# Two-layer hybrid attention trunk on one core: last feed-forward weights kept for the second token group, conditions loaded at their first use, the output projection's second half reversed, GpSimd taken out of the layer change

## The chip, the core and the metric

The kernel runs on one core of a Trainium2 chip. The metric is the device time of one execution in microseconds (us). Before the change the median of three runs is 1992.61 us (1989.99 to 1995.05). One more execution was recorded by the hardware profiler; all rows quoted in this document as "before" come from it.

The engines are named as in the profile: PE is TensorE (PEld is its loading of weights, PEq its sequencer), DVE is VectorE, ACT is ScalarE, POOL is GpSimd, and SP is SyncE, whose queue issues nearly all of this kernel's DMAs, one after another.

## The reference

A trunk of two layers works on 512 latent tokens (a grid 64 wide) and 256 context tokens, of width 1024, in float32. One layer computes:

```
mod            = silu(c) @ w_mod + b_mod          # six vectors: shift, scale, gate, twice; the same from c_ctx for context
h              = rms_norm(x, norm1) * (1 + sc1) + sh1
qa,ka,va, gq,gk,gv, ga,gb = split(h @ w_in)       # 8 windowed heads; 8 query, 2 key/value heads; two gates
ya             = windowed attention(qa, ka, va; + context keys, + position bias)
yb             = attention(rope(norm(gq)), rope(norm(gk)), gv; + context keys)
x              = x + g1 * ((sigmoid(ga) * (ya @ w_pa) + sigmoid(gb) * (yb @ w_pb)) @ w_o)
a, u           = split((rms_norm(x, norm2) * (1 + sc2) + sh2) @ w_ffn_in)      # 2816 columns each
x              = x + g2 * ((silu(a) * u) @ w_ffn_out)
```

Latent queries read their own keys and all context keys in one softmax; context tokens go through the same weights, and their result is needed up to the keys and values of the second layer. A last RMS norm follows.

## The kernel before, in words

**Products.** PE's fast float32 form keeps fewer bits than float32, so each operand is split into a high and a low part, and each product is made of three (high by high, high by low, low by high; `steps`, L369 to L381, the matmuls at L377). A weight comes through `weight` (L356): `raw` loads it in one DMA on the SP queue into one of four buffers `wr`, ACT copies the high part `wh` (L362), and DVE or POOL subtracts it to leave the low part `wl` (L364). There are three buffers each for `wh` and `wl`. A weight block of 1024 columns is 512 KB; eight blocks of 128 rows make one output block (24 matmuls for 512 tokens). Larger tiles live in a pool of 45 equal slots of 128 by 768 (`slot`, `spool`).

**Stages of a layer.** `mixing` makes the projections and attention; `merge` makes the gates (a projection each with weights from `win`) and the two branch projections (`pp`); `out_proj` multiplies by w_o (`po`, L1582 on) and adds to `x`; then the norm before the feed-forward; `ffn`; and `following`, the norm of the next layer. In layer 0 the spans hold latent and context tokens, in layer 1 latent ones alone.

**Order of the work.** In `mixing` PE's order is written out by a planner. It keeps a clock in us, knows what the other engines owe (`go` charges an operation to an engine; `plan["load"]` is the lead given to a weight), and picks between attention's own steps and projections that fill the gaps (`fill` in the two dictionaries, one for each layer). A step can state the time from which it may run (`Until`), and `ready["h"]` is that time for the context half of `h`. The other engines' instructions, and the whole order outside `mixing`, come from a scheduler which lays the instructions out by a simulation of its own, in the order in which the code issues them unless an operand is late.

**The layer change.** Layer 1 has the context's norm still to do when its latent tokens are ready. The leading projections (`prologue`) are the grouped keys (`late_k`), the first two query heads (`gqa_q` 0) and the grouped values (`late_v`), for latent tokens first. The weights of keys and values come through `kept` (L1253), which splits them in two pieces on ACT and DVE each into four of the eight `pt` tiles that attention uses later for the transposed probabilities; there they stay until context's turn. `late_norm` then makes the context half of `h` (L1284 sets its time), after which keys and values of the context follow. Other weights come through `load` (L759): in layer 1 it takes DVE for the subtraction as long as the planner's clock is below 8, and POOL afterwards. The rotary step (L770 to L776) multiplies by the cosine and adds on DVE, and multiplies by the sine on POOL (L774). The normalised keys are split on DVE (L1335); L799 is an ACT pass that empties a PSUM bank.

**The border to `merge`.** `run` calls `conditions` (L424 to L431) ahead of `merge`: it loads the condition vector, spread over 128 partitions (`crow`, 512 KB; two of them in layer 0), and applies silu with one ACT pass and two DVE passes (L435 to L437). The first gate weight and the `yb` tiles, which attention wrote to memory, are loaded after it. The users of `crow` are `mod_one` (L442): one block of `w_mod` each, loaded into a `wr` buffer, multiplied and summed on DVE (L446). In layer 0 blocks 16 and up are made beside `merge`, `out_proj` and `ffn`, those of layer 1 (0 to 39) beside layer 0's `ffn`; in layer 1 only blocks 40 to 47 are left, beside its own `ffn`.

**The output projection** (L1577) takes the tokens in two halves. Each half goes over the eight output blocks j = 0 to 7, and both load and split all eight weights. After the first half its norm and its cuts for the feed-forward (`modulate_half`, `cut`) run on DVE and ACT beside the second half; `late` does the second half's norm, and the feed-forward's first products run beside that.

**The feed-forward** makes its first product with fewer multiplications by sums of quarters (`quad`, matmuls at L1682, weights split at L1573 and L1574, and the first blocks plain, `pf`). The second product goes by chunks of hidden blocks; the last chunk, of six, is done for one group of tokens after another (L1814 to L1829), so that the norm of the first group can begin while the second runs: tokens 0 to 512 and 512 to 768 (context) in layer 0, 0 to 256 and 256 to 512 in layer 1. Each group goes over the eight output blocks and loads and splits all eight weights of 384 KB.

Of the kernel before, what the change touches and what calls it, by code (L numbers as in the profile page):

```python
# [42 lines left out]
for _n in ORDER:  # L43
    for _j in range(COLS[_n][1]):
# [27 lines left out]
         busy=12, ctx=0.0, vat=(1, 1), load=2, qt=2, rx=2, slow=(1.1, 1.2, 1), banks="gst", lead=(2, 1, 2)),  # L72
# [3 lines left out]
         busy=2, ctx=1, vat=(1, 1), load=2.5, qt=2, rx=1, slow=(1, 1, 1), banks="tsg", lead=(2, 2, 1)),  # L76
# [251 lines left out]
class Trunk:  # L328
# [430 lines left out]
    def load(self, l, what, j):  # L759
        if l == 0 and (what, j) in (("gk", 0), ("gv", 0), ("gq", 0)):  # L760
            return None
        first = l == 1 and (not self.flow or self.flow.clock < 8.0)
        return self.weight(self.d["win"][l, BLOCK[what, j]], D, self.nc.vector if first else None)
# [6 lines left out]
    def rope(self, t, pool):  # L770
# [3 lines left out]
        nc.gpsimd.tensor_tensor(sh, sh, self.sin, op=ALU.mult)  # L774
# [478 lines left out]
    def kept(self, l, what):  # L1253

        nc = self.nc
        raw = self.raw(self.d["win"][l, BLOCK[what, 0]], D)
        hi, lo = [[self.att.tile([P, S], F32R, tag="pt", name=self.name(n)) for _ in range(2)] for n in ("kh", "kl")]
        for i in range(2):
            part = raw[:, i * S : i * S + S]
            nc.scalar.activation(hi[i], part, AF.Copy)  # L1260
            nc.vector.tensor_tensor(lo[i], part, hi[i][:].bitcast(F32), op=ALU.subtract)
        return Pieces(hi), Pieces(lo)

    def late_norm(self, l, h, at):
# [19 lines left out]
        self.ready["h"] = end  # L1284
# [7 lines left out]
    def late_k(self, l, h, pool, out):  # L1292

        nc = self.nc
        w = self.kept(l, "gk")
# [45 lines left out]
    def late_v(self, l, h, pool, out):  # L1341

        nc = self.nc
        w = self.kept(l, "gv")
# [22 lines left out]
    def mixing(self, l, h, last, at, todo, spare):  # L1367
# [12 lines left out]
        with ExitStack() as stack:  # L1380
# [5 lines left out]
            pool = self.att = _Bufs(pool_, dict(rx=plan["rx"], qt=plan["qt"], p=ATT_P, pt=ATT_PT))  # L1386
            if at.rest:
# [189 lines left out]
    def out_proj(self, l, merged, x, nh, pool, beside):  # L1577

        hf = [self.slot("hf") for _ in range(KB)]
        right = {}  # L1580
        for half in range(2):
            a, b = half * nh, half * nh + nh  # L1582
            acc = None
            for j in range(KB):
                w = self.weight(self.d["wo"][l, j], D, self.nc.vector)
# [144 lines left out]
    def ffn(self, l, right, late, x, spans, groups, nh, done, pool, beside):  # L1730
# [83 lines left out]
        chunk = (FB - LAST) // CHUNK  # L1814
        for a, b in groups:
            acc = None
            for j in range(KB):
                w = self.weight(d["wfo"][l, j, :, chunk * CHUNK * P :], LAST * P, nc.vector)
# [12 lines left out]
    def run(self):  # L1831
# [3 lines left out]
        with (  # L1835
# [23 lines left out]
            for l in range(DEPTH):  # L1859
# [7 lines left out]
                with (  # L1867
# [6 lines left out]
                    crow, junk = self.conditions(stack.enter_context(  # L1874
                        tc.tile_pool(name=f"c{l}", bufs=1, reuse_waits="tile")), 1 if last else 2)
                    one = lambda l, n: lambda: self.mod_one(l, n, crow, junk)
# [265 lines left out]
```

## Time and profile before

| what | value |
|---|---|
| median of three runs | 1992.61 us |
| profiled execution | 1994.68 us |
| its span, first to last instruction | 1992.9 us |
| mean granted PE clock | 0.990 |
| busy: PE, DVE, ACT, POOL | 97%, 75%, 48%, 12% of the span |
| moved by DMA | 220.31 MB, 111 GB/s |
| loads of w_o, of 512 KB | 32 |
| loads of the feed-forward's last weights, of 384 KB | 32 |
| loads of `crow`, of 512 KB | 3 |

A group's row names line, engine and operation, the output and the inputs by the program's names, the tile's shape and the count; then, after the bar, its busy time, the mean time of one in ns, and the idle time of the engine just before, with the instruction that ended it. A row in order of time starts with the start in us and the busy time. A row of the table by stretch starts with the two ends and the length; busy us and counts of the engines follow, then the granted clock (1.00 is full speed) and the DMA engines' share. A row of the waits names who waits for whom, then total us, the number of waits and the longest. The mean clock of 0.990 and PE's 97% are averages over stages; the holes are short and lie at the borders of stages.

### The profile page before, as it was taken

How to read it: one execution, taken by the hardware profiler on the slowest of the kernel's cores; microseconds unless marked ns; L12 is line 12 of the kernel's file. 1: busy time of each engine (PE TensorE's matmuls, PEld its weight loads, DVE VectorE, ACT ScalarE, POOL GpSimd, SP SyncE). 2: the span in 40 equal slices, each digit the busy share in tenths (PEclk: the TensorE clock that was granted, in tenths of full speed). 3: DMA queues.
4: the chain of work that ended last, by engine and by line, in shares of the span. 5: the costliest groups of instructions: out<-in, count | busy, mean ns of one | idle time of the engine just before them, and what ended most of it. 6: DMA issues, size and time to landing. Idle time of an engine off the chain costs nothing.

```text
span 1992.9 us, 31834 instructions
## 1 busy us (share of the span) xinstructions
PE 1932.7 (97%) x12330; PEld 1785.3 (90%) x12330; DVE 1499.2 (75%) x2827; ACT 963.6 (48%) x1860; POOL 232.2 (12%) x135
## 2 busy tenths in 40 slices
PE   8999999999999999999999998999989999999998
PEld 8989999888899999998999877889978989999997
DVE  7477887789679989787756676889455579867786
ACT  4466666642236524242424354666443455444554
POOL 0332222223200000000000031322300000000000
PEclk9999999999999999999999999999989989999999
DMA  8121112244462343546222521112123543333334
GB/s 320 43 59 51 49 59 62 75 148 164 150 236 85 107 146 104 162 150 199 64 85 70 158 91 43 46 48 80 59 88 111 186 148 117 115 97 107 96 114 130
DMA packets 74839, 220.31 MB, mean 111 GB/s; under 512 B 8896, under 2 KB 11072, under 8 KB 74688
## 3 DMA queue, kind: packets, MB, share of 16 engines
q1 hardware_dynamic: 74688, 218.28, 33.6%
q8 instruction: 97, 1.59, 0.3%
q14 instruction: 54, 0.44, 0.1%
HBM read 206.19 MB, written 6.82 MB: 107 GB/s over the span
## 4 chain that ended last, share of the span: by engine, by line
PE 58%; DVE 10%; DMA 5%; issue 3%; ACT 2%; POOL 0%; SPq 0%; DVEq 0%; POOLq 0%; ACTq 0%
PE po L377 18%; PE qu L1682 10%; PE pj L377 10%; PE qv L1682 5%; PE pp L377 4%; DMA wr<-wmodT 3%; PE pf L377 3%; PE qc L1682 2%; PE pv L940 1%; DVE w L1574 1%; DMA wr<-wfi 1%; DVE wr L446 1%; PE sc L1023 1%; PE y L1059 1%; PE tp L1049 1%
## 5 line engine op out<-in xcount | busy, mean ns | idle before, releaser
L362 ACT ACTIVATE wh<-wr 128x512 fp32r<-128x512 f32 (+2 forms) x233 | 197.7, 852 | 368.8 <-PE po L377 126.7
L1682 PE MATMUL qu<-r,w 128*128 128x384 f32 (+1 forms) x1872 | 293.2, 310 | 1.4 <-ACT tt L1689 1.2
L1682 PEld LDWEIGHTS qu<-r,w 128*128 128x128 f32 x1872 | 279.6, 189 | 5.7 <-ACT tt L1689 5.3
L377 PE MATMUL pj<-h,wh 128*128 128x512 f32 (+1 forms) x688 | 254.1, 369 | 12.3 <-ACT wh L362 8.3
L377 PE MATMUL pj<-h,wl 128*128 128x512 f32 (+1 forms) x688 | 243.9, 355 | 0.0
L377 PE MATMUL pj<-hl,wh 128*128 128x512 f32 (+1 forms) x688 | 243.8, 354 | 0.0
L1573 ACT ACTIVATE w<-wr 128x512 fp32r<-128x512 f32 x234 | 144.1, 626 | 119.9 <-PE po L377 26.2
L377 PE MATMUL po<-ph,wh 128*128 128x512 f32 (+1 forms) x576 | 197.7, 344 | 1.1 <-ACT wh L362 1.1
L377 PE MATMUL po<-ph,wl 128*128 128x512 f32 (+1 forms) x576 | 196.5, 342 | 0.3 <-DVE wl L364 0.2
L364 POOL TENSOR_TENSOR wl<-wr,wh 128x1024 fp32r<-128x1024 f32 (+1 forms) x68 | 151.0, 2223 | 392.9 <-ACT wh L362 392.8
L377 PE MATMUL po<-pl,wh 128*128 128x512 f32 (+1 forms) x576 | 196.2, 341 | 0.0
L364 DVE TENSOR_TENSOR wl<-wr,wh 128x512 fp32r<-128x512 f32 (+2 forms) x165 | 149.4, 910 | 43.2 <-ACT wh L362 37.7
L1574 DVE TENSOR_TENSOR w<-wr,w 128x512 fp32r<-128x512 f32 x234 | 158.4, 686 | 24.0 <-ACT w L1573 22.6
L377 PEld LDWEIGHTS pj<-h,wh 128*128 128x128 f32 x688 | 131.3, 191 | 27.5 <-ACT wh L362 8.7
L1682 PE MATMUL qv<-r,w 128*128 128x384 f32 (+1 forms) x936 | 151.2, 310 | 3.9 <-DVE tt L1996 3.9
L1564 DVE SCALAR_TENSOR_TENSOR x<-po,G,x 128x256 f32<-128x256 f32 (+3 forms) x168 | 98.1, 595 | 67.9 <-PE po L377 67.5
L377 PEld LDWEIGHTS pj<-h,wl 128*128 128x128 f32 x688 | 130.8, 190 | 18.4
L1682 PEld LDWEIGHTS qv<-r,w 128*128 128x128 f32 x936 | 140.9, 189 | 5.6 <-DVE tt L1996 5.5
L377 PEld LDWEIGHTS pj<-hl,wh 128*128 128x128 f32 x688 | 131.4, 191 | 13.6
L499 POOL TENSOR_TENSOR rs<-rs,expo 128x2 f32<-128x2 f32 (+2 forms) x8 | 6.8, 855 | 1133.0 <-DVE rs L498 1133.0
L999 ACT ACTIVATE pth<-tp 128x512 fp32r<-128x512 f32 x176 | 103.6, 595 | 66.3 <-PE tp L1049 37.6
L1000 DVE TENSOR_TENSOR ptl<-tp,pth 128x512 fp32r<-128x512 f32 x176 | 119.8, 685 | 15.1 <-ACT pth L999 13.4
(241 smaller groups left out, 4323.4 us busy)
## 6 DMA issues: line engine op xcount, KB each, us to landing
wr<-wfi SPq DMA_DIRECT2D x88, 512.0 KB, 3.3
wr<-wmodT SPq DMA_DIRECT2D x86, 512.0 KB, 3.4
wr<-win SPq DMA_DIRECT2D x68, 512.0 KB, 3.3
wr<-wo SPq DMA_DIRECT2D x32, 512.0 KB, 4.0
wr<-wfo SPq DMA_DIRECT2D x64, 256.0 KB, 2.7
wr<-wfo SPq DMA_DIRECT2D x32, 384.0 KB, 3.3
wr<-wp SPq DMA_DIRECT2D x32, 256.0 KB, 3.3
x<-x SPq DMA_DIRECT2D x16, 384.0 KB, 7.6
```

The costliest lines, as they stand in the source:

```text
L362: nc.scalar.activation(hi, raw, AF.Copy)
L364: (eng or nc.gpsimd).tensor_tensor(lo, raw, hi[:].bitcast(F32), op=ALU.subtract)
L377: nc.tensor.matmul(ps[:, : b - a], u[:, c], v[k][:, a:b], start=(k == 0 and i == 0), stop=(k == nk - 1 and i == 2),)
L446: nc.vector.tensor_tensor_reduce(w, w, crow[:, 0], 1.0, 0.0, ALU.mult, ALU.add, self.mod[l][:, 0, n : n + 1])
L940: nc.tensor.matmul(ps[:, t * 256 : t * 256 + 256], a[k][:, tok], b[:, c], start=(k == 0 and i == 0), stop=(k == KB - 1 and i == 2))
L999: nc.scalar.activation(hi, tp, AF.Copy)
L1000: nc.vector.tensor_tensor(lo, tp, hi[:].bitcast(F32), op=ALU.subtract)
L1023: nc.tensor.matmul(s[:, lo:up], qt[:, b * P : (b + 1) * P], kk[k][:, lo:up], start=(k == 0 and (b % 2 == 0 or lo > 0)), stop=(k == 1), ski ...
L1564: self.nc.vector.scalar_tensor_tensor(x[j][:, f:u], ps[:, f - a : u - a], self.G[l][i][:, s, j : j + 1], x[j][:, f:u], op0=ALU.mult, op1=A ...
L1573: nc.scalar.activation(t[:, :n], src, AF.Copy)
L1574: nc.vector.tensor_tensor(t[:, n : 2 * n], src, t[:, :n].bitcast(F32), op=ALU.subtract)
L1682: nc.tensor.matmul(banks[bank], u[:, c], v, start=(first and k == 0 and i == 0), stop=(k == kn - 1 and i == 2), skip_group_check=True)
```

## The change

Five edits:

- **Last feed-forward weights.** The eight weights of the last chunk are loaded and split for the first group only, into 16 of the 45 slots, and the second group uses them again.
- **Conditions.** `conditions` is no longer called ahead of `merge` but by the first `mod_one` after it: in layer 0 that is still in `merge`, in layer 1 it is in the feed-forward.
- **Output projection.** The second half goes from j = 7 down to 0. The weights 7, 6 and 5 of the first half are still in their buffers and are used again; 4 to 0 are loaded and split a second time.
- **GpSimd.** Each plan gets `quiet`: as long as the planner's clock is below it, the weights loaded through `load` and the sine product of the rotary step take DVE in place of POOL. In layer 1 it is 18, in layer 0 it is 0.
- **Kept tiles.** In layer 1 `spared=2` sends the first two weights that are loaded with a planner (gq1 and gb0) through `kept` into `pt` tiles, and `kept` now charges its passes to the planner. The grouped keys and values take the ordinary buffers `wh` and `wl` instead. The time from which the context half of `h` may be read is put 2.0 us later.

```diff
--- before.py
+++ after.py
@@ -69,11 +69,11 @@
     dict(fill=("nk0 nv0 nq0 gq1 gb0 gq2 gb1 gq3 gb2 gb3 nq1",
                "gb4 nk1 gb5 nq2 nk2 nv1 nq3 nk3 gb6 gb7"),
          early=0.9, reserve=8, hop=0.14, move=3.5, soon=0.5, keep=2,
-         busy=12, ctx=0.0, vat=(1, 1), load=2, qt=2, rx=2, slow=(1.1, 1.2, 1), banks="gst", lead=(2, 1, 2)),
+         busy=12, ctx=0.0, vat=(1, 1), load=2, qt=2, rx=2, slow=(1.1, 1.2, 1), banks="gst", lead=(2, 1, 2), quiet=0.0, spared=0),
     dict(fill=("gq1 gb0 nq0 nv0 gq2 gb1 gq3 gb2 nq1 nk0 gb3",
                "nk1 nk2 nq2 nv1 nk3 gb4 nq3 gb5 gb6 gb7"),
          early=0.8, reserve=2, hop=0.2, move=3, soon=0, keep=2,
-         busy=2, ctx=1, vat=(1, 1), load=2.5, qt=2, rx=1, slow=(1, 1, 1), banks="tsg", lead=(2, 2, 1)),
+         busy=2, ctx=1, vat=(1, 1), load=2.5, qt=2, rx=1, slow=(1, 1, 1), banks="tsg", lead=(2, 2, 1), quiet=18.0, spared=2),
 ]
 
 
@@ -759,7 +759,10 @@
     def load(self, l, what, j):
         if l == 0 and (what, j) in (("gk", 0), ("gv", 0), ("gq", 0)):
             return None
-        first = l == 1 and (not self.flow or self.flow.clock < 8.0)
+        if self.flow and self.spared:
+            self.spared -= 1
+            return self.kept(l, what, j)
+        first = l == 1 and (not self.flow or self.flow.clock < self.quiet)
         return self.weight(self.d["win"][l, BLOCK[what, j]], D, self.nc.vector if first else None)
 
     def go(self, *ops, at=None):
@@ -771,7 +774,7 @@
         nc = self.nc
         sh = self.att.tile([P, T], F32, tag="rx", name=self.name("sh"))[:, :S]
         nc.vector.stream_shuffle(sh, t[:, :S], [i ^ 1 for i in range(32)])
-        nc.gpsimd.tensor_tensor(sh, sh, self.sin, op=ALU.mult)
+        (nc.vector if self.flow.clock < self.quiet else nc.gpsimd).tensor_tensor(sh, sh, self.sin, op=ALU.mult)
         nc.vector.tensor_tensor(t[:, :S], t[:, :S], self.cos, op=ALU.mult)
         nc.vector.tensor_tensor(t[:, :S], t[:, :S], sh, op=ALU.add)
 
@@ -1250,15 +1253,16 @@
         return [self.gqa_k(l, h, joint, pool, at.kk), self.gqa_v(l, h, joint, pool, at.vv),
                 self.gqa_q(l, 0, h, spans, pool, at.gqs)]
 
-    def kept(self, l, what):
-
-        nc = self.nc
-        raw = self.raw(self.d["win"][l, BLOCK[what, 0]], D)
+    def kept(self, l, what, j):
+
+        nc = self.nc
+        raw = self.raw(self.d["win"][l, BLOCK[what, j]], D)
         hi, lo = [[self.att.tile([P, S], F32R, tag="pt", name=self.name(n)) for _ in range(2)] for n in ("kh", "kl")]
         for i in range(2):
             part = raw[:, i * S : i * S + S]
             nc.scalar.activation(hi[i], part, AF.Copy)
             nc.vector.tensor_tensor(lo[i], part, hi[i][:].bitcast(F32), op=ALU.subtract)
+        self.go(("a", D), ("v", D), at=self.flow.clock + self.plan["load"])
         return Pieces(hi), Pieces(lo)
 
     def late_norm(self, l, h, at):
@@ -1281,7 +1285,7 @@
             first = self.go(("v", CTX), at=end if k == 0 else None)
             end = self.go(("a", CTX), ("v", CTX), at=first)
         flow.took("t", first)
-        self.ready["h"] = end
+        self.ready["h"] = end + 2.0
 
     def rest_ready(self):
 
@@ -1292,7 +1296,7 @@
     def late_k(self, l, h, pool, out):
 
         nc = self.nc
-        w = self.kept(l, "gk")
+        w = self.load(l, "gk", 0)
         yield Until(0.0)
         kg = pool.tile([P, T], F32, tag="qt", name=self.name("kg"))
         sq = pool.tile([P, T], F32, tag="qt", name=self.name("sq"))
@@ -1341,7 +1345,7 @@
     def late_v(self, l, h, pool, out):
 
         nc = self.nc
-        w = self.kept(l, "gv")
+        w = self.load(l, "gv", 0)
         yield Until(0.0)
         vt = pool.tile([P, T], F32, tag="qt", name=self.name("vt"))
 
@@ -1384,6 +1388,8 @@
                     tc.tile_pool(name=f"ps{w}{l}", bufs=1, space=PSUM, reuse_waits="tile")) for w in plan["banks"]}
             pool_ = stack.enter_context(tc.tile_pool(name=f"att{l}", bufs=1, reuse_waits="tile"))
             pool = self.att = _Bufs(pool_, dict(rx=plan["rx"], qt=plan["qt"], p=ATT_P, pt=ATT_PT))
+
+            self.quiet, self.spared = plan["quiet"], plan["spared"]
             if at.rest:
                 todo = self.prologue(l, h, spans, spare, at)
                 for g in todo:
@@ -1577,12 +1583,15 @@
     def out_proj(self, l, merged, x, nh, pool, beside):
 
         hf = [self.slot("hf") for _ in range(KB)]
-        right = {}
+        right, ws = {}, {}
         for half in range(2):
             a, b = half * nh, half * nh + nh
             acc = None
-            for j in range(KB):
-                w = self.weight(self.d["wo"][l, j], D, self.nc.vector)
+            for j in range(KB)[:: 1 - 2 * half]:
+
+                if half == 0 or j < KB - 3:
+                    ws[j] = self.weight(self.d["wo"][l, j], D, self.nc.vector)
+                w = ws[j]
                 if half == 0 and beside and MODS[2][j]:
                     beside.pop(0)()
                 ps = self.ps("a", "po")[:, :nh]
@@ -1812,10 +1821,13 @@
             beside.pop(0)[1]()
 
         chunk = (FB - LAST) // CHUNK
+        kept, slots = [], _Bufs(None, {}, dict(we=self.spool))
         for a, b in groups:
             acc = None
             for j in range(KB):
-                w = self.weight(d["wfo"][l, j, :, chunk * CHUNK * P :], LAST * P, nc.vector)
+                if a == 0:
+                    kept.append(self.weight(d["wfo"][l, j, :, chunk * CHUNK * P :], LAST * P, nc.vector, slots))
+                w = kept[j]
                 ps = self.ps("a", "po")[:, : b - a]
                 drain(self.steps(ps, w, second[chunk], a, b, LAST))
                 self.residual(l, 1, ps, x, j, a, b)
@@ -1871,9 +1883,15 @@
                 ):
                     self.psum = dict(n=psn, a=psa)
                     slots = dict(acc=self.spool, sq=self.spool, u=self.spool)
-                    crow, junk = self.conditions(stack.enter_context(
-                        tc.tile_pool(name=f"c{l}", bufs=1, reuse_waits="tile")), 1 if last else 2)
-                    one = lambda l, n: lambda: self.mod_one(l, n, crow, junk)
+                    rows, conds = [], stack.enter_context(tc.tile_pool(name=f"c{l}", bufs=1, reuse_waits="tile"))
+
+                    def one(of, n):
+                        def run():
+                            if not rows:
+                                rows.extend(self.conditions(conds, 1 if last else 2))
+                            self.mod_one(of, n, *rows)
+                        return run
+
                     ahead = 40 if last else 16 + sum(sum(m) for m in MODS)
                     beside = [] if last else [one(0, n) for n in range(16, ahead)]
                     with tc.tile_pool(name=f"m{l}", bufs=1, reuse_waits="tile") as pool_:
```

## The prediction

> **What bounds the kernel.** I read the engines' busy time, then the table by stretch, then the waits, then the order of time where the table shows a hole. TensorE (PE) carries the kernel:
>
> ```profile
> span 1992.9 us, 31834 instructions
> PE 1932.7 (97%) x12330; PEld 1785.3 (90%) x12330; DVE 1499.2 (75%) x2827; ACT 963.6 (48%) x1860; POOL 232.2 (12%) x135
> ...
> 560.00:580.00 20.00, 20.00 (x118) 20.00 (x117) 16.65 (x29) 7.87 (x11) 0.00 (x0) 1.00 0.88 334
> ...
> 1149.60:1174.60 25.00, 23.43 (x89) 17.19 (x90) 18.30 (x29) 12.29 (x24) 5.66 (x3) 0.86 0.32 106
> 1174.60:1209.00 34.40, 28.03 (x153) 24.86 (x152) 25.01 (x45) 15.44 (x31) 14.20 (x8) 0.90 0.20 62
> 1240.00:1470.50 230.50, 225.75 (x1513) 203.40 (x1512) 177.62 (x404) 140.76 (x294) 59.80 (x35) 1.00 0.17 53
> 1470.50:1486.00 15.50, 7.19 (x20) 5.38 (x20) 7.15 (x11) 6.28 (x10) 0.00 (x0) 0.67 0.69 220
> 1600.00:1640.00 40.00, 35.83 (x261) 34.48 (x260) 30.68 (x58) 23.45 (x45) 1.01 (x2) 0.87 0.47 157
> ```
>
> After the length the columns are PE, weight loads, DVE, ACT and POOL, then the granted PE clock. The matrix products are untouched by the change, so time can only come from PE's holes, and from the slow clock that follows them. Three stretches hold them: the layer change (1149.6 to 1209), the border between attention and merge of layer 1 (1470.5), and the norm before layer 1's feed-forward (1600 to 1640). The longest wait of all and the one ahead of the feed-forward, in PE's list of waits:
>
> ```profile
> PE pj L377 <- ACT wh L362: 8.3, 1, 8.3
> ...
> PE pf L377 <- DVE r L1650: 3.8, 4, 1.2
> ```
>
> **Conditions at first use.** In layer 1 `conditions` stands ahead of `merge`. Its tile lies where attention's tiles lay, and the SP queue goes in order:
>
> ```profile
> SPq L429 <- DVE ptl L1000: 22.1, 1, 22.1
> ...
> 1444.45 0.54 SPq L1525 DMA_DIRECT2D yb<-yd  x1
> 1470.46 0.33 SPq L429 DMA_DIRECT2D crow<-crow  x1
> 1470.85 1.37 SPq L1525 DMA_DIRECT2D yb<-yd  x3
> 1472.32 0.38 SPq L353 DMA_DIRECT2D wr<-win  x1
> ...
> wr<-win SPq DMA_DIRECT2D x1, 512.0 KB, 6.0
> ...
> 1478.37 2.10 ACT L362 ACTIVATE wh<-wr 128x1024 fp32r<-128x1024 f32 x3 [0.69 <-DMA wr<-win]
> ...
> 1470.78 0.39 PE L377 MATMUL pj<-h,wl 128*128 128x512 f32 x1
> 1479.48 0.79 PE L377 MATMUL pj<-h,wh 128*128 128x512 f32 x1 [8.31 <-ACT wh L362]
> ...
> 1484.76 0.50 PE L377 MATMUL pj<-h,wl 128*128 128x512 f32 x1
> ```
>
> The load of `crow` waits 22.1 us for attention's last split, and behind it in the queue wait three `yb` loads and the first gate weight (`win`). That weight is issued at 1472.32, lands 6.0 us later, is split on ACT, and PE, which had ended at 1471.17, begins again at 1479.48: 8.3 us. Then 12 products take 5.28 us (1479.48 to 1484.76), 0.44 each, at a granted clock of 0.67 over the stretch; elsewhere such a product starts every 0.227 us (rows 1171.19 and 1171.42 below). That is 2.6 us more, 10.9 in all. With the load gone from there, the weight can go out when attention still runs. What is late next are the other three `yb`: if their slots too come free only at 1470.85, they land some 5 us later, 1476, and their four splits follow, while the first gate product holds PE for 24 x 0.227 = 5.4 us, to 1476.6. I leave 1.4 us for that: **9.5 us**, bounds 0 (another buffer holds the weight) and 10.9.
>
> The conditions do not vanish. Layer 1 then does them in the feed-forward or wherever the schedule finds SP free: one 512 KB load, one ACT and two DVE passes, priced by
>
> ```profile
> L435 ACT ACTIVATE junk<-crow 128x1024 f32<-128x1024 f32 x3 | 3.2, 1058 | 5.8 <-DMA crow<-crow 3.7 <-DVE crow L437 2.0
> ...
> L436 DVE SCALAR_TENSOR_TENSOR junk<-junk,crow 128x1024 f32<-128x1024 f32 x3 | 3.7, 1226 | 5.9 <-DMA yb<-yd 3.0 <-ACT junk L435 2.9
> ...
> L437 DVE TENSOR_SCALAR crow<-junk 128x1024 f32<-128x1024 f32 x3 | 2.1, 692 | 0.1
> ...
> L1759 ACT ACT_TABLE_LOAD x2 | 2.6, 1283 | 0.0
> ...
> 1624.04 1.23 DVE L446 CUSTOM_DVE_ANT_0 wr<-wr,crow 128x1024 f32<-128x1024 f32 x1 [0.67 <-DMA wr<-wmodT]
> ```
>
> The last row is the first user of `crow`: DVE waits there 0.67 us for a DMA, amid the splits for which PE waits 3.8 us. If the conditions come right ahead of it, they add 1.06 + 1.23 + 0.69 = 3.0 us, and up to two table loads (their Tanh among the Silus), 2.6: a loss of 5.6. Against that, PE's waits there of 3.8 us and a clock of 0.87 leave up to 6 us to win, because the reversed half takes work away just before. In layer 0 conditions and users stay in the same stretch of the merge: 0. The trace can't say where the scheduler puts them; I take **0**, bounds -5.6 and +6.
>
> The Trainium skill speaks against this edit: "ScalarE: Activation LUTs", section "What ACT_TABLE_LOAD costs", charges some 2.66 us for every switch of set, the drain included. By it the two switches would cost 5.3 us instead of the 2.6 of the rows; the trace agrees with its 1283 ns for the load itself, and no row here shows the drain.
>
> **Reversed second half.** Weights 7, 6 and 5 are kept: per layer three loads, three ACT and three DVE splits fewer. PE was full there, so the removed work was hidden already: **0** by itself. No new wait: weight 4 takes the buffer of 7, free one product into the half, and has two products' time to be split, as every weight has now.
>
> **Last feed-forward weights kept.** In layer 0 the second group (context) loads and splits the same eight weights again (768 columns: DVE 0.96). Its products are not the loss; what stands behind them on DVE, SP and the weight buffers is: the norm and the weights of layer 1.
>
> ```profile
> L364 DVE TENSOR_TENSOR wl<-wr,wh 128x1024 fp32r<-128x1024 f32 x53 | 64.6, 1222 | 11.0 <-ACT wh L362 10.5
> ...
> L364 DVE TENSOR_TENSOR wl<-wr,wh 128x768 fp32r<-128x768 f32 x32 | 30.2, 955 | 7.0 <-ACT wh L362 6.2 <-ACT ph L1768 0.9
> ...
> L524 DVE SCALAR_TENSOR_TENSOR hl<-u,mod,h 128x512 fp32r<-128x512 f32 x8 | 6.0, 748 | 2.6 <-ACT h L523 2.6
> L522 DVE SCALAR_TENSOR_TENSOR u<-x,A,rb 128x512 f32<-128x512 f32 x8 | 5.9, 742 | 0.0
> ...
> 1149.62 0.50 PE L377 MATMUL pj<-h,kh 128*128 128x512 f32 x1 [1.82 <-ACT kh L1260]
> ...
> 1171.19 0.39 PE L377 MATMUL pj<-hl,kh 128*128 128x512 f32 x1
> 1171.42 0.39 PE L377 MATMUL pj<-h,kl 128*128 128x512 f32 x1
> ...
> 1173.69 0.95 PE L787 MATMUL st<-hones,sq 128*128 128x2 f32 x8
> ```
>
> PE waits 1.82 us for the first key weight, then the three leading projections (72 products, 16.3 us at 0.227) last from 1149.62 to 1173.69, 24.1 us: they follow DVE, which makes `h` in pieces. Loss: 9.6 us. The change frees 8 x 0.96 = 7.6 us of DVE just before, and SP and the buffers, so that the weights of k, q and v can be ready before the norm starts. DVE then owes from the norm's start, some 10 us before 1149.62, the norm's 11.9 us, 2.4 for the two weights in pieces and five residuals under 0.69, about 17 us, to 1157; PE, beginning at 1147.8 (1149.62 less 1.82) and doing 9 x 0.227 = 2 us per piece, needs the last of eight pieces at 1162. So nearly all could come back; I take **7 us** of 9.6, bounds 0 and 9.6. In layer 1 the second group feeds nothing but the end: 0. The kept tiles take 16 of 45 slots; the group's products free two every 2 us, faster than the norm asks, so 0.
>
> **GpSimd out of the layer change.** In 1174.6 to 1209 PE waits 6.4 us for a bank that ACT and, behind a full DVE queue, the query split empty late:
>
> ```profile
> 1188.90 2.40 POOL L364 TENSOR_TENSOR wl<-wr,wh 128x1024 fp32r<-128x1024 f32 x1 [2.90 <-ACT wh L362]
> ...
> 1189.89 1.97 DVE L776 TENSOR_TENSOR kg<-kg,sh 128x512 f32<-128x512 f32 x1
> ...
> 1201.44 0.69 DVE L776 TENSOR_TENSOR qg<-qg,sh 128x512 f32<-128x512 f32 x1
> ...
> L775 DVE TENSOR_TENSOR qg<-qg,cos_sb 128x512 f32<-128x512 f32 x2 | 4.4, 2222 | 0.0
> ...
> L1335 DVE TENSOR_TENSOR kk<-kg,kk 64x512 fp32r<-64x512 f32 x4 | 4.9, 1230 | 0.1
> ...
> 1203.59 0.58 PE L377 MATMUL pj<-h,kh 128*128 128x256 f32 x1 [6.37 <-ACT kg L799]
> ```
>
> The same DVE addition takes 0.69 us alone and 1.97 beside a POOL split, ending just after that ends. With 0.69 for every pass of 512 columns, DVE loses over these rows 1.3 + 2 x 1.53 + 4 x 0.54 = 6.5 us. The change puts one weight (1.22) and two or three rotations (0.69 each) on DVE, 2.6 to 3.3: net 3.2 to 3.9 us of DVE. PE's loss is the 6.4 and, at a granted clock of 0.90 over 34.4 us, at most 3.4 more: 9.8. I take **3 us**, about what DVE gains, bounds -3.3 and 9.8. What is new: the weights of k and v now hold two of the three `wh`/`wl` buffers until context's turn, so `nv0`'s second weight waits for it, on POOL as before.
>
> The Trainium skill, "SBUF — State Buffer", section "SBUF: two separate sides", says that the loser of the port pair shared by these two engines fully blocks; the trace agrees (0.69 becomes 1.97). By it, `nv0`'s two splits, 2.4 us each, could still cost DVE 4.8.
>
> **Sum.** 9.5 + 0 + 0 + 7 + 3 = 19.5 us from the profiled execution's 1994.7 (span 1992.9 and 1.8 around it): 1975.2. The median of the runs, 1992.6, lies 2.1 below that execution: **1973**.
>
> **Rivals.** (1) Layer change given back: context's norm still ends when it did, PE only arrives earlier and waits with one weight buffer left; for it speaks that `nv0` has no other buffer, against it that DVE has 10 us less to do. 1973 + 10 = 1983. (2) The border keeps its wait, because a weight buffer or bank is late too: 1973 + 9.5 = 1982.5; against it, one `yb` load did go at 1444.45. (3) The conditions fall into the norm at 1620: 5.6 us, and 4.4 for landing: 1983. (4) Slower: layer 1's PE order is planned anew from other due times (`h` 2 us later, kept weights charged). Its 230 us of attention have 4.8 us of holes (225.75 of 230.5). If the new order fits as badly as the stretch 1174.6 to 1209 did (6.4 in 34.4, so 43 us in 230), it loses 38: 1973 + 38 = 2011. It decides once half of the stage fits that badly, since 20 us of new holes cancel the sum. Against it: the plan's costs after 18 us of its clock stay what they were. (5) The change doesn't do what it says, the loads stay where they were in the queue: 1992.
>
> **Chances.** Forecast 0.60 (own range 1961 to 1981), (1) 0.17, (2) 0.08, (3) 0.06, (4) 0.06, (5) 0.03. About 0.3%, 6 us, is what a measurement here can tell from none: faster means under 1986.6. The forecast and (1) to (3), 0.91, lie there but for their edges: 0.86. The edges (0.05) and (5) make same 0.08; slower 0.06. Range: all upper bounds together, 10.9 + 9.6 + 9.8 + 6 = 36, give 1956; the border alone less 5.6 gives 1989. I take 1960 to 1990.
>
> **What would show it.** Right: the `crow` load no longer waits between 1444 and 1470, no 8.3 us wait after attention, and the clock at the border stays near 1. The leading projections take under 18 us; DVE's `kk` splits 0.7 us each. 384 KB loads fall from 32 to 16, `wo` loads from 32 to 26. Wrong: a new PE wait for `nv0` or for context's keys in the layer change, table loads beyond four, or more than 10 us of holes in layer 1's attention.

## The result and the profile after

The changed kernel takes 2036.6 us (median of four runs, 2035.41 to 2041.08) against 1992.82 us before: a ratio of 1.0225, 95% interval 1.0204 to 1.0245. The forecast of 1973 us was wrong in sign: the change loses 44 us. Ratios here and below leave out one outlier, one of twelve executions of the layer change's edit alone, which took 6707.7 us.

The head of the profiled execution's page, and the first rows of PE's list of waits, after:

```profile
span 2034.4 us, 31690 instructions
...
PE 1951.3 (96%) x12330; PEld 1794.1 (88%) x12330; DVE 1484.2 (73%) x2809; ACT 946.2 (47%) x1838; POOL 224.9 (11%) x131
```

```profile
PE po L377 <- ACT wh L362: 28.8, 15, 2.5
PE po L377 <- ACT ph L1777: 4.8, 2, 2.7
...
PE po L377 <- DVE wl L364: 3.1, 10, 0.5
...
PE pj L377 <- ACT kg L802: 1.7, 1, 1.7
```

The first products of `po` with a weight, as a group on the page of before; the last column is PE's idle time ahead of them:

```profile
L377 PE MATMUL po<-ph,wh 128*128 128x512 f32 (+1 forms) x576 | 197.7, 344 | 1.1 <-ACT wh L362 1.1
```

DVE, ACT and POOL have less to do than before and PE makes the same 12330 products, yet PE waits longer: fifteen waits of the output product `po` for the high part of a weight, 28.8 us, where before there were 1.1 us in all. The waits of `po` for `ph` are new too. The waits that the prediction worked on (8.3 us behind `crow`, 6.4 us for `kg`) are gone or down to 1.7.

To see where the 41.5 us between the two spans (1992.9 and 2034.4) went, I took the first or last start of groups of PE's products as marks and subtracted. `pp` are the branch products, the sums are those of squares for a norm, the scores `sc` and the outputs `y` belong to attention (the last `y` here and below is that of the grouped heads; the windowed heads follow it), `pf` and `qu` are the feed-forward's first products and `po` its second. Each column is a stretch in us:

| kernel | layer 0's first `pp` to the sums for layer 1's norm | sums to first scores | scores to last `y` | to first `pp` | `pp` | to last `pf` | to last `qu` | to last `po` | to the end |
|---|---|---|---|---|---|---|---|---|---|
| before | 706.2 | 85.7 | 139.5 | 121.8 | 89.3 | 92.1 | 283.5 | 36.5 | 11.0 |
| after | 741.4 | 73.7 | 139.9 | 118.3 | 82.2 | 91.6 | 283.0 | 67.2 | 11.3 |

The first stretch runs from 427.3 to 1133.5 before and from 425.8 to 1167.2 after. Two stretches lose, 35.2 and 30.7 us, and both end with the last chunk of a feed-forward, the place where the weights are now kept. Three win: 12.0 us in the layer change, 3.5 and 7.1 on either side of the border. The grouped heads take the same within 0.4 us, and the whole of attention, from the first score to the last `y` of the windowed heads, 251.9 us for 251.0. (The marks of one execution scatter by some 2 us in the layer change: two kernels below that do not touch it show 83.4 and 83.6 for the 85.7.)

The last chunk by stretch, before (layer 0's first group, then the whole of layer 1's chunk):

```profile
1090.30:1129.00 38.70, 38.70 (x174) 31.47 (x173) 20.16 (x28) 13.48 (x20) 0.00 (x0) 1.00 0.48 148
...
1945.40:1982.20 36.80, 35.87 (x294) 35.05 (x293) 27.57 (x49) 20.57 (x39) 1.36 (x1) 1.00 0.47 144
```

and after (the first group in layer 0, then in layer 1, then the second group in layer 1):

```profile
1101.70:1157.80 56.10, 39.13 (x130) 28.38 (x131) 19.72 (x24) 12.71 (x17) 0.00 (x0) 0.82 0.37 120
...
1961.40:2005.00 43.60, 29.68 (x129) 26.60 (x130) 12.19 (x20) 8.04 (x14) 0.00 (x0) 0.63 0.10 27
2005.00:2023.20 18.20, 18.20 (x149) 18.20 (x148) 8.73 (x18) 6.19 (x16) 0.70 (x1) 0.96 0.18 58
```

PE was full there before. After, it is idle for 17.0 and 13.9 us of the first group's stretches, and the granted clock there is 0.82 and 0.63 on average. The second group, which loads nothing, is full again. So the kept weights hurt in the group that loads them, not in the one that reuses them. ACT, DVE and PE in that stretch, in order of time:

```profile
1111.48 0.63 ACT L477 ACTIVATE sq<-x 128x512 f32<-128x512 f32 x1 [7.64 <-DVE x L1570]
1112.02 0.83 ACT L362 ACTIVATE wh<-wr 128x768 fp32r<-128x768 f32 x1
1118.70 0.63 ACT L477 ACTIVATE sq<-x 128x512 f32<-128x512 f32 x1 [5.85 <-DVE x L1570]
1119.23 0.83 ACT L362 ACTIVATE wh<-wr 128x768 fp32r<-128x768 f32 x1
```

```profile
1117.91 0.75 DVE L1570 SCALAR_TENSOR_TENSOR x<-po,G,x 128x512 f32<-128x512 f32 x1 [4.07 <-PE po L377]
```

```profile
1112.90 0.50 PE L377 MATMUL po<-ph,wh 128*128 128x512 f32 x1 [2.24 <-ACT wh L362]
...
1120.11 0.50 PE L377 MATMUL po<-ph,wh 128*128 128x512 f32 x1 [2.24 <-ACT wh L362]
```

ACT has nothing to do for 5.85 us, then makes the square of the finished block (`sq`, for the next norm) and only after that the high part of the next block's weight. The weight itself had been in its `wr` buffer since before 1090: four `wfo` loads went out between 1071.06 and 1086.57, and the last of them landed at 1089.29. So every block goes round one loop: PE's 18 products, the residual on DVE at 1117.91, the square at 1118.70, the split at 1119.23, and PE again at 1120.11. The loop takes 7.2 us (1112.90 to 1120.11) where the products alone take some 4.2 (18 of them, some 0.23 us apart). Before, ACT in the same place splits three weights ahead of the first pass over a finished block, and later ones ahead of the square:

```profile
1106.15 2.31 ACT L362 ACTIVATE wh<-wr 128x768 fp32r<-128x768 f32 x3 [4.75 <-PE po L377]
1108.37 0.61 ACT L474 ACTIVATE acc<-x 128x512 f32<-128x512 f32 x1
...
1112.83 0.85 ACT L362 ACTIVATE wh<-wr 128x768 fp32r<-128x768 f32 x1 [2.79 <-issue]
1113.80 0.63 ACT L477 ACTIVATE sq<-x 128x512 f32<-128x512 f32 x1
```

### The profile page after: what moved, and what is told of

It reads as the page before. It is cut to its first block, busy times and chain, and to the rows that moved or that the text cites. A ratio compares the mean times of both kernels' runs of the same rounds, so it can differ in the third digit from the quotient of the medians.

```text
span 2034.4 us, 31690 instructions
## 1 busy us (share of the span) xinstructions
PE 1951.3 (96%) x12330; PEld 1794.1 (88%) x12330; DVE 1484.2 (73%) x2809; ACT 946.2 (47%) x1838; POOL 224.9 (11%) x131
## 4 chain that ended last, share of the span: by engine, by line
PE 58%; DVE 10%; DMA 4%; ACT 3%; issue 2%; POOL 0%; DVEq 0%; POOLq 0%; ACTq 0%
PE po L377 19%; PE qu L1691 11%; PE pj L377 9%; PE qv L1691 5%; PE pp L377 4%; DMA wr<-wmodT 3%; PE qc L1691 3%; PE pf L377 2%; DVE wr L446 1%; DVE w L1580 1%; PE pv L943 1%; DVE wl L364 1%; PE sc L1026 1%; ACT wh L362 1%; PE y L1062 1%
## 5 line engine op out<-in xcount | busy, mean ns | idle before, releaser
L362 ACT ACTIVATE wh<-wr 128x1024 fp32r<-128x1024 f32 (+2 forms) x211 | 178.0, 846 | 312.0 <-PE po L377 97.9
L377 PE MATMUL po<-ph,wh 128*128 128x512 f32 (+1 forms) x576 | 208.4, 362 | 33.6 <-ACT wh L362 28.8
L377 PE MATMUL po<-ph,wl 128*128 128x512 f32 (+1 forms) x576 | 206.1, 358 | 3.1 <-DVE wl L364 3.1
L377 PE MATMUL po<-pl,wh 128*128 128x512 f32 (+1 forms) x576 | 204.8, 356 | 0.8 <-DVE pl L1778 0.8
L1580 DVE TENSOR_TENSOR w<-wr,w 128x512 fp32r<-128x512 f32 x234 | 158.3, 686 | 24.2 <-ACT w L1579 22.6
L377 PEld LDWEIGHTS po<-ph,wh 128*128 128x128 f32 x576 | 116.2, 202 | 51.8 <-ACT wh L362 33.9
L364 DVE TENSOR_TENSOR wl<-wr,wh 128x512 fp32r<-128x512 f32 (+2 forms) x144 | 128.3, 894 | 44.6 <-ACT wh L362 39.6
L377 PEld LDWEIGHTS pj<-h,wh 128*128 128x128 f32 x704 | 133.0, 189 | 22.5 <-ACT h L523 2.6
L377 PEld LDWEIGHTS po<-ph,wl 128*128 128x128 f32 x576 | 115.6, 201 | 21.9 <-DVE wl L364 7.8
```

The lines of the kernel that those rows point to most:

```text
L362: nc.scalar.activation(hi, raw, AF.Copy)
L364: (eng or nc.gpsimd).tensor_tensor(lo, raw, hi[:].bitcast(F32), op=ALU.subtract)
L377: nc.tensor.matmul(ps[:, : b - a], u[:, c], v[k][:, a:b], start=(k == 0 and i == 0), stop=(k == nk - 1 and i == 2),)
L1580: nc.vector.tensor_tensor(t[:, n : 2 * n], src, t[:, :n].bitcast(F32), op=ALU.subtract)
```

## The experiments

**Theory.** The kept tiles come from the pool of 45 slots, under the one tag from which the squares and their sum come too. The tiles of one tag are handed out in the order in which the code first writes them. Then the tile for the split of weight j+1 can't be given before that of the square of block j, and the scheduler places the split behind the square on ACT. Before, the weights had tags of their own. **Rival A:** 16 kept tiles beside the others are too many for 45 slots, and weights wait for slots to come free. **Rival B:** another edit costs the 44 us. The runs form three groups of four, each beside runs of the kernel before on the same chip (medians 1995.4, 1993.8 and 1993.8 us), so ratios are compared.

**The last weights not kept.** The changed kernel, less this edit:

```diff
-                if a == 0:
-                    kept.append(self.weight(d["wfo"][l, j, :, chunk * CHUNK * P :], LAST * P, nc.vector, slots))
-                w = kept[j]
+                w = self.weight(d["wfo"][l, j, :, chunk * CHUNK * P :], LAST * P, nc.vector)
```

> The changed kernel, but the last feed-forward weights are loaded for both groups as before. Theory (one line of tiles): the kept weights and the squares of x take tiles from one pool under one tag, handed out in the order of the code, so the split of weight j+1 stands behind the square of block j on ACT; all the loss, 36 us in layer 0 and 31 us in layer 1, is there. Then this kernel has none of PE's waits po <- ACT wh (28.8 us in 15), and the 22 us that the layer change, attention and border gained remain but for up to 7: 1965 to 1977 us. Rival A (too few slots): the same time here. Rival B (the new plan or the moved conditions cost it): over 2000 us.

Measured: 1979.94 us, ratio 0.992 (0.9906 to 0.9933); profiled 1976.5. The longest wait of `po` for `wh` is 0.7 us, and all three make 1.4. The time lies 3 us above the expected range, which was written when before stood at 1992.8 us; 0.992 of that is 1977, its upper end.

**Only the last weights kept,** on the kernel before (the same lines, the other way round).

> The kernel before with only the kept feed-forward weights. Theory (one line of tiles) and rival A (too few slots): 1993 + 36 + 31 = 2060, less up to 10 us that the layer change finds ready: 2050 to 2062 us, with PE's waits po <- ACT wh near 29 us. Rival B (another edit costs it): under 1995 us.

Measured: 2055.73 us, ratio 1.0296 (1.028 to 1.0313). PE's list of waits:

```profile
PE po L377 <- ACT wh L362: 28.9, 15, 2.6
PE pj L377 <- ACT wh L362: 8.1, 1, 8.1
PE pj L377 <- ACT kg L799: 5.8, 1, 5.8
```

The new wait of 28.9 us stands beside the two old ones. These two runs settle that this edit alone makes the loss and that the other four together gain: rival B falls.

**Weights three products ahead.** Same tiles, same slots; the code only asks for each weight earlier:

```diff
-                if a == 0:
-                    kept.append(self.weight(d["wfo"][l, j, :, chunk * CHUNK * P :], LAST * P, nc.vector, slots))
+                while a == 0 and len(kept) < min(KB, j + 3):
+                    i = len(kept)
+                    kept.append(self.weight(d["wfo"][l, i, :, chunk * CHUNK * P :], LAST * P, nc.vector, slots))
```

> The changed kernel, with each kept weight loaded and split three products ahead in the order of the code; the same 16 of 45 slots are used. Theory (one line of tiles): the splits now stand ahead of the squares, PE's waits po <- ACT wh fall from 28.8 us to under 3, and the time is that of the kernel that does not keep them, less 0 to 7 us for the work saved: 1960 to 1975 us. Rival A (too few slots): the slots come free no earlier, the waits stay over 15 us and the time over 2000 us.

Measured: 1980.34 us, ratio 0.9919 (0.9906 to 0.9933), as without the edit. The waits of `po` for `wh` are 3.0 us in 3. The number of slots is the same, and rival A (waits over 15 us, over 2000 us) falls here. The further 0 to 7 us that I expected for the work saved did not come.

**The squares' tile from another tag.** Nothing loaded ahead; the square of the last chunk takes one of the feed-forward's own tiles:

```diff
-                    acc = self.square(x[j], a, b, pool, acc)
+                    acc = self.square(x[j], a, b, _Bufs(None, {}, dict(acc=self.spool, sq=Sevens(pool, nh))), acc)
...
+class Sevens:
...
+    def tile(self, shape, dt, tag=None, name=None):
+        return self.pool.tile([P, 2 * self.nh], dt, tag="ps", name=name)
```

> The changed kernel, with the tile of the squares in the last chunk taken from another tag (the feed-forward's own tiles for hidden blocks), nothing loaded ahead in the code. Theory (one line of tiles): only weight 1 still stands behind an ACT pass, the one that fills the sum of squares from block 0, because that tile is still a slot; so one wait of about 3 us in each layer, and the time 1965 to 1982 us. Rival A (too few slots): one slot less is in use out of 45, so most of the waits stay: over 2010 us.

Measured: 1987.0 us, ratio 0.9957 (0.9944 to 0.9969). ACT in order of time, layer 0:

```profile
1087.06 0.83 ACT L362 ACTIVATE wh<-wr 128x768 fp32r<-128x768 f32 x1
...
1105.65 0.63 ACT L474 ACTIVATE acc<-x 128x512 f32<-128x512 f32 x1 [3.09 <-DVE x L1570]
1106.19 3.03 ACT L362 ACTIVATE wh<-wr 128x768 fp32r<-128x768 f32 x4
1111.30 1.78 ACT L362 ACTIVATE wh<-wr 128x768 fp32r<-128x768 f32 x2 [2.08 <-DMA wr<-wfo]
...
1116.66 0.64 ACT L477 ACTIVATE sq<-x 128x512 f32<-128x512 f32 x1 [0.25 <-DVE x L1570]
```

This is the run that names the cause. The sum of squares `acc` is still a slot, and weight 1 still stands behind it. The squares are slots no more, and the weights behind weight 1 stand behind none of them: they are split as they land, ahead of the first square. The order of the code is that of the changed kernel, and so, but for one, is the number of slots: rival A falls again, and it is the shared tag that puts the splits behind the squares. How the pool then orders its tiles is inferred from these runs. The time missed its expectation (1965 to 1982, written when before stood at 1993; here it is 1995): I priced the one wait that stays in each layer at 3 us, but the sums come 10.1 us later than without the edit (1143.8 against 1133.7), and layer 1's chunk takes 41.4 in place of 36.5. Most of the 10.1 us can be read from the trace: PE waits 2.7 us for `ph` and 2.2 for weight 1, and from 1102.12 to 1112.36 the granted clock is 0.50, which over 7.31 busy us costs 3.7 by an estimate. Without the edit PE is full there at a clock of 1.00 (48.99 of 49 us from 1085 to 1134).

**Weights five ahead** (`j + 5` for `j + 3`).

> As the kernel that loads the kept weights three products ahead, but five. Theory: at three, weight 3 still stood behind the pass that opens the sum of squares, PE waited 1.3 us there and filled in with products of the second group, so that the norm began 4.6 us later. At five that wait goes and the first group runs unbroken: the norm's sums start 2 to 4 us earlier, and the time is 0 to 4 us under the kernel with three ahead: 1973 to 1980 on the scale of the last call. Rival (the norm's own chain sets the end): the sums come earlier, the first scores don't, the time is the same within 1 us.

Measured: 1973.95 us, ratio 0.9897 (0.9881 to 0.9913). ACT:

```profile
1085.50 0.83 ACT L362 ACTIVATE wh<-wr 128x768 fp32r<-128x768 f32 x1
...
1087.01 2.31 ACT L362 ACTIVATE wh<-wr 128x768 fp32r<-128x768 f32 x3
1090.44 0.85 ACT L362 ACTIVATE wh<-wr 128x768 fp32r<-128x768 f32 x1 [1.12 <-DMA wr<-wfo]
...
1111.84 0.63 ACT L474 ACTIVATE acc<-x 128x512 f32<-128x512 f32 x1 [1.95 <-DVE x L1570]
```

Five weights are split before the sum of squares opens, and the waits of `po` for `wh` are down to 1.3 us in 2. The sums come at 1133.0 (1138.3 with three ahead). The first scores come 3.4 us earlier (1210.2 for 1213.6), so the rival for this run, that the scores would not move, falls.

**One edit alone,** on the kernel before, for the other edits and for the kept weights without their stall (five ahead).

> The kernel before with only the conditions called at first use. Theory: the border from attention to merge loses its wait of 8.3 us and its slow clock, some 10.6 us as in the run that keeps no weights, and the conditions' passes in the norm of layer 1 cost nothing: 10 us under the kernel before, ratio 0.993 to 0.996. Rival (the passes cost in the norm what was won at the border): ratio 0.998 to 1.000, with the stretch from the last pp to the last pf longer than 92.1 us by 5 or more.

> The kernel before with only the two plans' new entries, the kept tiles for gq1 and gb0, and the later time of h. Theory: the stretch from the norm's sums to the first scores falls from 85.7 us by 5 to 9 (PE's wait of 6.4 us for the bank that kg empties late goes), the border keeps its 8.3 us: ratio 0.995 to 0.998. Rival (what was won in the layer change came from the other edits): ratio 0.999 to 1.002 and the stretch over 83 us.

> The kernel before with only the output projection's second half reversed and three weights reused. Theory: PE was full there, so the three loads and six passes that go away in each layer were hidden: ratio 0.999 to 1.001; the stretch from the last pp to the last pf (92.1 us) shortens by at most 1.5. Rival (the reversed order makes the sum of squares or the norm later): ratio 1.001 to 1.004.

> The kernel before with only the kept feed-forward weights, loaded five products ahead. Theory: without the stall the edit is worth 1.9 us in the second group of layer 1 (36.5 to 34.6 us from the last qu to the last po) and 0 to 3 us in the layer change, since the norm of layer 1 goes by its own chain of slots: ratio 0.9975 to 0.9995. Rival (the 7 us of the forecast were there and the layer change's new plan took them away): ratio 0.995 to 0.9965 and the stretch from the norm's sums to the first scores under 80 us.

| edit alone | ratio (interval) | us of 1993.8 | sums to first scores | last `y` to last `pp` | last `qu` to last `po` |
|---|---|---|---|---|---|
| none (before) | 1 | 0 | 85.7 | 211.1 | 36.5 |
| conditions at first use | 0.9952 (0.9935 to 0.9968) | -9.6 | 83.4 | 200.3 | 36.4 |
| GpSimd out, kept tiles, later `h` | 0.9971 (0.996 to 0.9982) | -5.8 | 78.0 | 211.3 | 36.4 |
| reversed half | 0.9996 (0.9988 to 1.0005) | -0.8 | 83.6 | 211.3 | 36.5 |
| last weights kept, five ahead | 0.9968 (0.9955 to 0.9981) | -6.4 | 80.3 | 210.9 | 34.6 |

The conditions are worth 10.8 us at the border and give back nothing that exceeds the scatter. The layer change's edit takes 7.7 us off its stretch, as expected, and the reversed half is worth nothing. The kept weights came out between the two cases written down for them: a ratio just under the theory's, the stretch at 80.3 just over the rival's bound. Alone, the edits add up to 22.6 us; together, without the stall, they are worth 20.5 (ratio 0.9897). So together they are worth about what they are alone. The layer change's 7.7 us are 5.5 against the 83.4 and 83.6 of the two kernels that leave that stretch as it was; its ratio says 5.8.

**The norm's rows ahead.** If tiles are handed out so, the norm of layer 1 should show the same fault: its row `u` and both parts of `h` are slots, written in the order u, h, hl. DVE in the kernel with weights five ahead:

```profile
1153.78 0.74 DVE L522 SCALAR_TENSOR_TENSOR u<-x,A,rb 128x512 f32<-128x512 f32 x1
1155.31 0.75 DVE L524 SCALAR_TENSOR_TENSOR hl<-u,mod,h 128x512 fp32r<-128x512 f32 x1 [0.79 <-ACT h L523]
1155.98 0.74 DVE L522 SCALAR_TENSOR_TENSOR u<-x,A,rb 128x512 f32<-128x512 f32 x1
1157.52 0.75 DVE L524 SCALAR_TENSOR_TENSOR hl<-u,mod,h 128x512 fp32r<-128x512 f32 x1 [0.79 <-ACT h L523]
```

DVE waits for ACT in five of the eight pieces, 0.79 us in three of them, with the next `u` free to be made; in the other three it has other work. The edit writes that next `u` first:

```diff
+        us = []
         for k in range(KB):
-            self.modulate(l, i, k, x, rb, a, b, h, pool)
+            while len(us) < min(KB, k + 2):
+                us.append(self.scaled(l, i, len(us), x, rb, a, b, pool))
+            self.modulate(l, i, k, x, rb, a, b, h, pool, us[k])
```

> The same, and in the norm of layer 1 the scaled row u of piece k+1 stands ahead of the passes that make h and hl of piece k in the code. Theory (one line of tiles, handed out in the order of first writing): u, h and hl are all slots, so u of the next piece waited for hl of this one, and a piece took DVE 0.74 + ACT 0.72 + DVE 0.74 = 2.2 us; now DVE alone sets 1.5 us, eight pieces take 12 us in place of 17.6, and the time is 3 to 6 us under the kernel with five ahead. Rival (DVE's other work or the weight splits fill the 0.8 us anyway, or PE's products set the pace): within 1.5 us of it.

Measured: 1969.96 us, ratio 0.9882 (0.9866 to 0.9899). DVE now:

```profile
1143.55 0.74 DVE L518 SCALAR_TENSOR_TENSOR u<-x,A,rb 128x512 f32<-128x512 f32 x1
1144.21 0.75 DVE L531 SCALAR_TENSOR_TENSOR hl<-u,mod,h 128x512 fp32r<-128x512 f32 x1
1144.88 0.74 DVE L518 SCALAR_TENSOR_TENSOR u<-x,A,rb 128x512 f32<-128x512 f32 x1
```

The norm takes 14.9 us (1139.63 to 1154.5) in place of 19.6 (1138.66 to 1158.27), and the stretch from the sums to the first scores falls from 77.2 to 71.6. The median is 4.0 us lower, though the two intervals overlap; the stretch is what shows the effect. This edit moves the pass in the code as well, so, unlike the squares' tag, it does not tell the order of the tiles from the order of the code.

**The same on the kernel before.**

> The kernel before with only the scaled row of piece k+1 ahead of h and hl of piece k in the norm of layer 1. Theory (one line of tiles): the chain of 2.2 us a piece goes, but DVE still splits the second group's weights then, so 2 to 5 us of the 85.7 are won: ratio 0.9973 to 0.999. Rival (DVE is full there, the chain costs nothing): 0.9995 to 1.0005.

Measured: 1989.1 us, ratio 0.9978 (0.9968 to 0.9988). The stretch falls to 79.0, but in the profiled execution, which at 1993.94 us is the slowest of the runs, the sums come 5.6 us later, and why is open. The verdict rests on the runs.

**Layer 1's conditions between merge and output projection,** on top of the best kernel:

```diff
+                        if last:
+                            rows.extend(self.conditions(conds, 1))
                         x = []
```

> The kernel with weights five ahead and the norm's rows ahead, and layer 1's conditions computed between the merge and the output projection instead of at the first use. Theory: at the first use the two DVE passes of 1.22 and 0.69 us stand in the norm ahead of the feed-forward, where PE waits 1.8 us for a cut; between merge and projection DVE has room, so 1 to 2 us go: ratio to the kernel before 0.9865 to 0.988. Rival (other DVE work takes the place): 0.988 to 0.989, as the kernel without it.

Measured: 1967.36 us, ratio 0.987 (0.9857 to 0.9883), the fastest of all. The passes move from 1598 and 1600 to 1525 and 1526, where DVE has room. From the last `pp` to the last `pf` takes 90.6 us for 91.9. The median is 2.6 us lower, which the intervals alone don't separate from none.

## Why the prediction was wrong

**The step that failed** is "The kept tiles take 16 of 45 slots; the group's products free two every 2 us, faster than the norm asks, so 0", with "In layer 1 the second group feeds nothing but the end: 0". I counted slots and priced the group that reuses the weights. What moves is the group that loads them: its weights change their tag, and with it their place in the order on ACT. That cost 66 us in two places (35.2 and 30.7), where the forecast had put this term at 0. The slots were never what was short: the same 16, asked for five products ahead, leave 1.3 us of these waits. None of the signs that I named for "wrong" lay in this stretch, and no rival did: the slower one, a badly replanned attention, did not happen (251.0 us for the whole of attention before, 251.9 after). The before trace held a hint that I read past: the norm's wait of `hl` for `h` (2.6 us, in the last four of its eight pieces), with the next `u` not made.

**Conditions, 9.5 us: right.** 10.8 us in the stretch, 9.6 by the ratio, near the upper bound of 10.9. SP's order of time after shows it, with PE's first branch product `pp` at 1499.1:

```profile
1485.02 1.81 SPq L1531 DMA_DIRECT2D yb<-yd  x4
1495.03 0.33 SPq L353 DMA_DIRECT2D wr<-wp  x1
1495.45 0.38 SPq L429 DMA_DIRECT2D crow<-crow  x1
```

```profile
1485.00:1505.00 20.00, 20.00 (x108) 17.13 (x107) 10.42 (x21) 9.48 (x19) 0.00 (x0) 1.00 0.42 132
```

All four `yb` go out together and PE has no hole. The 1.4 us that I kept back for the `yb` splits was not needed. `crow` itself is loaded at 1495, long before its use at 1632 (ACT) and 1633 (DVE); the passes fell into the norm, as rival (3) said, but cost about 1.3 us there (91.9 us against 90.6 with the passes moved ahead) and not 10. ACT_TABLE_LOAD stays at four, so the switches that the Trainium skill, "ScalarE: Activation LUTs", section "What ACT_TABLE_LOAD costs", charges for did not occur; its 2.66 us is not tested here.

**Reversed half, 0: right** (0.9996, interval across 1). The loads of w_o fell from 32 to 26, those of 384 KB from 32 to 16, as written.

**Kept weights, 7 us of gain: the size was near, partly by luck, and could not be reached in this form.** Without the stall they are worth 6.4 us alone (0.9968): in the profiled execution 5.4 us in the layer change (3 against the two kernels at 83.5) and 1.9 in layer 1's second group, which I had put at 0. The sign that I had named, leading projections under 18 us, did not come: from the first key product to the sums behind them (24.1 us before, 22.5 in the two kernels that leave this stretch alone) they take 22.6 after and 20.2 with the kept weights alone. They take 17.3 with the norm's rows ahead as well, and 18.9 with those rows ahead alone. So the norm's own order seems to have held them up more than the weights did.

**GpSimd out, 3 us: too small.** The edit is worth 5.8 us by the ratio and 5.5 to 7.7 in its stretch. The run holds the kept tiles and the later `h` too, so what GpSimd alone is worth is not separated. With this edit alone, two rows of the groups of the layer change, and two of PE's list of waits there:

```profile
L1339 DVE TENSOR_TENSOR kk<-kg,kk 64x512 fp32r<-64x512 f32 x4 | 2.7, 682 | 0.1
L1317 DVE COPY rx<-hr 128x256 f32<-128x256 f32 x1 | 2.5, 2491 | 1.2 <-POOL hr L793 1.2
```

```profile
PE pj L377 <- ACT kg L802: 1.7, 1, 1.7
PE pj L377 <- DVE hl L524: 1.6, 1, 1.6
```

The splits `kk` are down to 0.68 us each and PE's wait for the bank from 6.4 to 1.7. I took DVE's net gain as PE's, where PE's own loss (6.4 us and the slow clock behind it) would have come nearer. The contention is not gone, only moved to where less hangs on it: the copy `rx` of 128 by 256 takes 2.49 us, where the same copy of twice its width takes 0.43 in this trace, beside the POOL split of 2.41 us that starts at 1202.65. That agrees with the Trainium skill, "SBUF — State Buffer", section "SBUF: two separate sides": the loser blocks fully.

So the sum of 19.5 us was nearly what the edits give when the weights are loaded ahead (20.5), and the one edit that changed a tile's tag turned it into a loss of 44. That the two sums lie so close is in part luck: the layer change was worth more than I put, and the edits alone add up to 22.6.

## What to carry to other kernels

When an edit moves a tile to another pool or tag, list what else takes tiles there and in which order the code first writes them: a tile that depends on nothing can then come behind one that waits for the end of the previous step. Sharing a tag costs order, not only room; if it must be shared, ask for the early tiles some steps ahead in the code, and look for engines that sit idle for one operation in every step of a loop. When an edit removes work, check that the work that stays still starts when it did.

## What was not expected of the hardware

In layer 1, waits of some 2 us, one after another, cost PE nearly as much again in clock. Layer 1's first group after, one block of it by stretch and in order of time:

```profile
1968.00:1974.50 6.50, 4.58 (x18) 3.99 (x18) 1.87 (x3) 1.14 (x2) 0.00 (x0) 0.50 0.22 61
```

```profile
1969.19 0.58 PE L377 MATMUL po<-ph,wh 128*128 128x256 f32 x1 [1.76 <-ACT wh L362]
...
1970.56 0.41 PE L377 MATMUL po<-ph,wh 128*128 128x256 f32 x1
1970.77 0.41 PE L377 MATMUL po<-pl,wh 128*128 128x256 f32 x1
...
1975.72 0.58 PE L377 MATMUL po<-ph,wh 128*128 128x256 f32 x1 [1.76 <-ACT wh L362]
```

PE is idle for 1.76 us a block, and the granted clock is 0.50 over the whole of it. The products start 0.21 us apart; before, at a clock of 1.00, 294 of them take 35.87 us, 0.122 each. Over the first group the clock is 0.63: by an estimate its 29.7 busy us hold about 18.7 at full speed, so 11 us of the loss there are clock, beside 13.9 of waits. In layer 0, with longer products between the waits, the clock is 0.82 and, by the same estimate, some 7 us go that way, beside 17.0 of waits. The Trainium skill, "TensorE: Matmul & The Clock Gate", section "HAM oscillation — how this bites in real kernels", gives as its abstract rule that PE should have no idle gaps over about 3.4 us. By that rule these gaps would be harmless; the trace differs, and the measurement decides: gaps of 1.76 us, one in every 6.5 us, went with a clock of 0.50 for 17 us (1962.2 to 1979.2). Neither the length of a gap nor the share of idle time settles the clock, though: in layer 0 PE was idle for 2.24 us of every 7.21 (1112.90 to 1127.32) at a clock of 1.00. What decides between the two, no run here shows.
